# First stage of a two-block kernel: the copies of the turned tables and ScalarE's sign of them become two steps a round apart, modulation goes ahead of the powers, weights are split one step ahead

## The chip, the cores and the metric

One core of a Trainium2 chip runs the whole program; the other seven are idle. The metric is device microseconds (us) of one execution. The engines are PE (TensorE, matmuls), DVE (VectorE), ACT (ScalarE), POOL (GpSimd) and SP (SyncE, which issues nearly all DMAs). Each works through its own instructions in order and waits on semaphores.

## What is computed

Two transformer-like blocks on 512 positions of 1,024 channels in float32. The change lies in the first mixer of the first block, a state-space mixer (S5), and in the work before it:

```python
def modulate(x, g, shift, scale):
    return rmsnorm(x, g) * (1.0 + scale) + shift
...
    u = h @ w_in
...
    lb_re = mag * jnp.cos(lim * dt)
    lb_im = mag * jnp.sin(lim * dt)
...
    def chunk_step(carry, u_c):
        bu_re = jnp.einsum('blgc,gpc->blgp', u_c, bb_re)
...
        _, _, hs_re, hs_im = lax.associative_scan(combine, (a_re, a_im, bu_re, bu_im), axis=1)
        y = jnp.einsum('blgp,gcp->blgc', hs_re, cr) - jnp.einsum('blgp,gcp->blgc', hs_im, ci)
```

There are 64 groups of 16 channels, each with 64 complex states. Later come a gated output, a gated MLP, attention, and a second block with two more attentions and MLPs; nothing of that is touched.

## The kernel before

**The first stage** (the block that begins at line 729) treats the 64 groups in eight units of eight groups. Positions are taken eight at a time, so that the recurrence has 64 steps with the eighth power of the state's factor. A unit n passes through steps, each named by a letter and the unit's number:

- W splits the unit's slice of `s5_w_in` into a high part (`whi`, ACT, L271) and a low part (`wlo`, POOL, L272; unit 0's on DVE); G is the projection of 24 matmuls (L378 to L380, three products of eight slices), its copy `sq` (ACT, L921) and the store `ud` (SP); L loads it back as `U`.
- K (ACT, L951 to L955) signs the unit's constants; F (DVE, L979 to L984) and C (POOL, L967 to L969) make its two tables `bt` and `cp`.
- P (PE, L1004) turns `bt`, and ACT copies it to `bp` (L1005); Q (PE, L1013 and L1016; ACT `lags`, L1018) and A (eight DMAs, L1023) make the table `T` of short lags.
- R makes rotations for two units (DVE, L934 to L936, six operations); **U** (`turns`, L986 to L997) copies a unit's rotations to both halves of the partitions, tile `ecs` (two DMAs of 256 KB, L993), and then ACT signs the half `es` (L994) and fills `d` for the scan (L997).
- I (PE, L1034; ACT, L1037) is the input to the states; **S** (DVE, L1044 to L1047: a product with `ec`, one with `es`, a sum, the scan; ACT, L1050: exchange of halves; DVE, L1052) the recurrence; B (DVE, L1058 and L1059) turns the states back; O (PE, L1067 and L1069; ACT, L1072, the gelu `dg`; a store) is the output.

The order of all these steps is written out by hand in the string ORDER (L76), one line for each round, and a loop (L1168) issues them; PE, DVE and POOL keep that order, ACT keeps it within this block. SP's queue is put in order by the framework's scheduler. In round n stand S, B and O of unit n, and P, Q, A and I of unit n+1, beside W of n+4 and G of n+3:

```python
         "S1 W5 F3 B1 C3 P2 G4 Q2 A2 I2 O1 U3 L3 K4 "
         "S2 W6 F4 B2 C4 P3 G5 Q3 A3 I3 O2 R2 U4 L4 K5 "
```

Tiles rotate through few buffers: two of `ecs`, of `whi`, of `wlo` and of PSUM `mm`, three of PSUM `s`.

**Ahead of the rounds**, DVE makes the exponentials and sines; the constants of the input table (`den` to `kim`, L834 to L846); the normalised input `hnl` (L854); the eighth power of `mag` (L860); and from it the powers of the rotations, `up` (L871 to L875). Then come the modulation's `m_ada` and `A` (L1109, L421), and for each of eight slices `split_x` (ACT L901 and L905, DVE L903 and L906), which gives the operands of G0. Beside the splits the table `few` of small rotations is built, by a list `lf` of operations that are merged between them (recorded operations all have line L721). POOL makes the powers `LR`, `LI`, then `KR`, `KI` (L1106 to L1108), then C of unit 0.

**After the rounds** the gated output goes on with `cb`, a broadcast of `c` that takes over the buffer of `few` (load L125, silu on ACT L126).

Of the kernel before, what the change touches and what calls it, by code (L numbers as in the profile page):

```python
# [9 lines left out]
F32 = mybir.dt.float32  # L10
F32R = mybir.dt.float32r
I32 = mybir.dt.int32
AF = mybir.ActivationFunctionType
OP = mybir.AluOpType
# [4 lines left out]
P = 128  # L19
D = 1024  # L20
S = 512
KD = D // P
# [6 lines left out]
C1 = 6.28125  # L29
C2 = 0.0019350051879882812  # L30
C3 = TWO_PI - C1 - C2
# [21 lines left out]
def _consts():  # L53
# [19 lines left out]
C_DVE, BC_BUFS = 0, 3  # L73
Z_POOL, W_ADD, SUMS_POS, SPREAD_POS, GATE_RATE = 0, 'dve', 12, 22, 1.3
T_ACT, MERGE_AT = 0, 50
ORDER = ("G0 W1 G1 F0 L0 P0 K1 W2 R0 G2 Q0 A0 C1 F1 L1 W3 U0 I0 U1 K2 "  # L76
# [8 lines left out]
LAG_BUFS, U_BUFS, U_ACT, W_DVE, LO_POOL, BC_POS, XR, NORM_POOL, V_DVE, SP_ORDER = 2, 3, 0, 0, 0, 4, 0, 8, 0xaa, 2  # L85
EARLY = 6
# [5 lines left out]
def tile_two_blocks(ctx, tc, ap, out):  # L92
    nc = tc.nc
    pe, act, dve, pool = nc.tensor, nc.scalar, nc.vector, nc.gpsimd

    hp = ctx.enter_context(tc.tile_pool(name="hp", bufs=1))
    hnp = ctx.enter_context(tc.tile_pool(name="hnp", bufs=KD))
# [4 lines left out]
    ps_mm = ctx.enter_context(tc.tile_pool(name="ps_mm", bufs=2, space=PSUM))  # L102
# [313 lines left out]
    h = [hp.tile([P, S], F32, name=f"h{k}") for k in range(KD)]  # L416
# [306 lines left out]
    def merge(*lists):  # L723

        todo = sorted(((i + 0.5) / len(l), n, i) for n, l in enumerate(lists) for i in range(len(l)))
        for _, n, i in todo:
            lists[n][i]()

    with tc.block(schedule_with_timeline_sim=TIMELINE):
# [39 lines left out]
        def part(i):  # L769
            k, j = divmod(i, 4)  # L770
            raw = hnp.tile([P, S], F32, name="hnh")
            nc.sync.dma_start(raw, ap["ada_w0"][k * P:(k + 1) * P, j * S:(j + 1) * S])
            pe.matmul(rows[32 * j:32 * j + 32], cz[:, k, :], raw, start=k == 0, stop=k == KD - 1)
        norm, ln = Norm(KD, pool), Later(dve)
# [14 lines left out]
        def sm(n):  # L789
            return sc.tile([P, NG], F32, name="sm_" + n)  # L790
        dt, mag, th, x, x2 = sm("dt"), sm("mag"), sm("th"), sm("x"), sm("x2")
# [39 lines left out]

        KR, KI = (sc.tile([P, NG, 8], F32, name=n) for n in ("KR", "KI"))
        kre, kim, den, nre = sm("kre"), sm("kim"), sm("den"), sm("nre")
        dve.tensor_tensor(den, lre, lre, OP.mult)  # L834
        dve.tensor_tensor(x2, lim, lim, OP.mult)
        dve.tensor_tensor(den, den, x2, OP.add)
# [8 lines left out]
        dve.tensor_tensor(kim, kim, x2, OP.subtract)  # L845
        dve.tensor_tensor(kim, kim, den, OP.mult)  # L846

        for i in range(SUMS_POS, SPREAD_POS):
            part(i)
        rb = norm.spread(ps_mm, "mm")  # L850
        hs = []
        for k in range(KD):
            t = hnp.tile([P, S], F32, name="hnl")
            dve.tensor_tensor(t, h[k], rb, OP.mult)  # L854
            hs.append(t)

        for _ in range(3):
            dve.tensor_tensor(mag, mag, mag, OP.mult)  # L860
        pows = [sc.tile([P, 3, NG], F32, name=f"up{i}") for i in range(3)]
        for half in range(2):
            r = HALF[half]
# [2 lines left out]
            act.activation(to[:, 0], cs3[r, 1:3, gs], AF.Copy)  # L866
            act.activation(to[:, 1], sn3[r, 1:3, gs], AF.Copy, scale=-1.0)
            act.activation(to[:, 2], sn3[r, 1:3, gs], AF.Copy)
        ut = sm("ut")
        for c, nx in zip(pows, pows[1:]):  # L870
            dve.tensor_tensor(ut, c[:, 2, :], c[:, 2, :], OP.mult)  # L871
            dve.tensor_tensor(nx[:, 0, :], c[:, 0, :], c[:, 0, :], OP.mult)
            dve.tensor_tensor(nx[:, 0, :], nx[:, 0, :], ut, OP.subtract)
            for j in (1, 2):
                dve.scalar_tensor_tensor(nx[:, j, :], c[:, 0, :], 2.0, c[:, j, :], op0=OP.mult, op1=OP.mult)  # L875
# [20 lines left out]
        def split_x(k):  # L896
            hi, lo = hnp.tile([P, S], F32R, name="hnh"), hnp.tile([P, S], F32R, name="hnl")
            X.append((hi, lo))
            a, b = A[:, k:k + 1], B[:, k:k + 1]
            v = tmp.tile([P, S], F32, name=f"t{k % 4}")  # L900
            act.activation(hi, hs[k], AF.Identity, bias=b, scale=a)  # L901
            if V_DVE >> k & 1:
                dve.tensor_scalar(v, hs[k], a, b, op0=OP.mult, op1=OP.add)  # L903
            else:
                act.activation(v, hs[k], AF.Identity, bias=b, scale=a)  # L905
            (pool if LO_POOL >> k & 1 else dve).tensor_tensor(lo, v, hi.bitcast(F32), OP.subtract)  # L906
# [34 lines left out]
        class Tables:  # L941
# [44 lines left out]
            def turns(self):  # L986
                i = self.i
                e = E[i % 4]
                ecs = sp.tile([P, 2, G8, 64], F32, name="ecs")
                self.ec, self.es = ecs[:, 0], ecs[:, 1]  # L990
                src = HALF[i // 4]
                for r in HALF:
                    nc.sync.dma_start(ecs[r], e[src])  # L993
                act.activation(self.es, self.es, AF.Identity, scale=sgn[:, 0:1])  # L994
                self.d0 = d0s[order.index(i) % 2]
                gs = slice(i * G8, (i + 1) * G8)
                act.activation(self.d0[:, :, 1:], mag[:, gs, None].to_broadcast([P, G8, 63]), AF.Copy)  # L997
# [87 lines left out]
        tabs, U = [], []  # L1085
        bsp = ps_a.tile([P, S], F32, name="aux")
        tabs.append(Tables(0))
        lf = Later(dve)
        et = ps_s.tile([P, 2, NG, 4], F32, name="s")
        lf.memset(few[:, 0, :, 0:1], 1.0)  # L1090
        lf.memset(few[:, 1, :, 0:1], 0.0)
# [11 lines left out]
        for x, y, z, op in ((KR, kre, kim, OP.subtract), (KI, kim, kre, OP.add)):  # L1103
            sh = [P, NG, 8]
            t = tmp.tile(sh, F32, name="t0")
# [7 lines left out]
        split_x(1)  # L1113
        wt = split_w(0, dve)
        tabs[0].for_c(pool)
        for x, y in zip(turn_by, pows):
            act.activation(x, y, AF.Copy)
        merge([lambda k=k: split_x(k) for k in range(2, KD)], lf.ops)
        weights_of, sab, wz, w_of, wg = {0: wt}, {}, {}, {}, {}
        tabs, U = [tabs[0]] + [None] * (KD - 1), [None] * KD  # L1120
        Y, glu = [None] * KD, {}
# [33 lines left out]
        def do_glu(m, i):  # L1155
            if not i:
                glu[m] = ps_mm.tile([P, S], F32, name="mm")
            k = order[i]
            cs_ = slice(k * P, (k + 1) * P)
            mm3(glu[m], wg[m][0][:, cs_], wg[m][1][:, cs_], *Y[k], i == 0, i == KD - 1)  # L1160
# [1 line left out]
            "K": do_tables, "F": lambda n: tabs[n].for_b(dve), "C": lambda n: tabs[n].for_c(dve if C_DVE >> n & 1 else pool),  # L1162
            "W": do_w, "G": lambda n: gather(n, weights_of.pop(n)), "P": lambda n: tabs[n].on_pe(), "Q": lambda n: tabs[n].for_lags(), "L": do_u,
            "I": do_inputs, "S": do_states, "B": do_back, "A": lambda n: tabs[n].toeplitz(), "O": do_outputs,
            "R": do_rotations, "U": lambda n: tabs[n].turns(), "Y": do_y, "v": do_glu_w,
            "a": lambda i: do_glu(0, i), "b": lambda i: do_glu(1, i),
        }
        for step in ORDER.split():  # L1168
            steps[step[0]](int(step[1]))
# [12 lines left out]
        for m in range(KD):  # L1182
# [7 lines left out]
            y = tmp.tile([P, S], F32, name="t1")  # L1190
# [4 lines left out]
        norm = Norm(KD)  # L1195
# [70 lines left out]
    norm = nxt  # L1266
# [99 lines left out]
    norm = Norm(KD)  # L1366
# [19 lines left out]
    norm = nxt  # L1386
# [3 lines left out]
    W2 = ap["a_wqkv_2"]  # L1390
# [36 lines left out]
    norm = Norm(KD)  # L1427
# [25 lines left out]
    norm = nxt  # L1453
# [126 lines left out]
    norm = Norm(KD)  # L1580
# [138 lines left out]
```

## Time and profile before

| | us |
|---|---|
| median of 3 runs (2684.5, 2689.98, 2694.06) | 2689.98 |
| the profiled execution | 2683.22 |
| its span, first to last instruction | 2681.3 |
| busy in the span: PE / DVE / ACT / POOL | 2519.2 / 1737.9 / 1148.6 / 357.4 |

PE is busy for 94% of the span. In the page's 40 slices of 67 us it has 4, 8, 7 and 6 tenths in the first four and 9 in nearly all that follow, and the clock that TensorE was granted is 8, 7, 8 and 6 tenths of full speed in these four and 9 later. So the first 270 us are where PE waits, and they are read by stretches, by the waits there, and by the instructions in order of time.

### The profile page before, as it was taken

The numbers are of one execution on the slowest core, as the hardware profiler recorded it, in microseconds if no ns is written. First come the engines' busy times: TensorE is split into PE (matmuls) and PEld (weight loads), VectorE is DVE, ScalarE is ACT, GpSimd is POOL, SyncE is SP. The second block draws the span as 40 slices with busy tenths as digits, with TensorE's granted clock in tenths as the row PEclk, the third lists the DMA queues.
The fourth block names the chain that finished last, engine by engine and source line by source line (L and its number), as shares of the span: only waits on it lengthen the run. The fifth ranks groups of instructions, "written<-read, shape, count | busy, mean of one in ns | idle before, by whom it ended". The sixth has DMA issues, their size and how long they took to land. (4 is left out here: it accounts for less than half of the span.)

```text
span 2681.3 us, 32817 instructions
## 1 busy us (share of the span) xinstructions
PE 2519.2 (94%) x12098; PEld 2015.6 (75%) x12098; DVE 1737.9 (65%) x3111; ACT 1148.6 (43%) x1925; POOL 357.4 (13%) x346
## 2 busy tenths in 40 slices
PE   4876989999999999999999999999999889999998
PEld 1665778888877767888887877788888667788887
DVE  8654886455577668646568566985766776753554
ACT  3443344233355554323335554532434576542342
POOL 4441100000022210000012110550000220000000
PEclk8786989999999999999999999999999899999999
DMA  5443655354433235546433333455543112223322
GB/s 207 114 118 103 214 194 164 113 164 132 121 102 103 91 122 158 166 147 194 146 117 118 97 109 126 146 153 169 173 141 109 31 32 87 87 85 105 95 82 75
DMA packets 131120, 335.67 MB, mean 125 GB/s; under 512 B 37008, under 2 KB 41872, under 8 KB 130960
## 3 DMA queue, kind: packets, MB, share of 16 engines
q1 hardware_dynamic: 129232, 331.74, 40.3%
q8 instruction: 95, 1.56, 0.2%
q10 hardware_dynamic: 1728, 1.84, 0.2%
q14 instruction: 65, 0.53, 0.1%
HBM read 320.68 MB, written 6.29 MB: 122 GB/s over the span
## 5 line engine op out<-in xcount | busy, mean ns | idle before, releaser
L272 DVE TENSOR_TENSOR wlo<-wraw,whi 128x1024 fp32r<-128x1024 f32 (+4 forms) x424 | 464.5, 1096 | 419.6 <-ACT whi L271 414.1
L271 ACT ACTIVATE whi<-wraw 128x1024 fp32r<-128x1024 f32 (+4 forms) x431 | 408.0, 948 | 744.7 <-PE mm L379 551.0
L378 PE MATMUL mm<-hnh,whi 128*128 128x512 f32 x1152 | 467.3, 406 | 33.4 <-ACT whi L271 22.0
L379 PE MATMUL mm<-hnl,whi 128*128 128x512 f32 x1152 | 462.9, 402 | 9.0 <-POOL hnl L296 4.0
L380 PE MATMUL mm<-hnh,wlo 128*128 128x512 f32 x1152 | 459.6, 399 | 4.8 <-POOL wlo L272 3.9
L378 PE MATMUL mm<-g,whi 128*128 128x512 f32 (+1 forms) x922 | 360.1, 391 | 6.3 <-ACT g L271 3.1
L380 PE MATMUL mm<-g,wlo 128*128 128x512 f32 (+1 forms) x922 | 359.3, 390 | 0.0
L379 PE MATMUL mm<-g,whi 128*128 128x512 f32 (+1 forms) x922 | 359.2, 390 | 0.0
L378 PE MATMUL s<-hnh,whi 128*128 128x512 f32 x720 | 288.2, 400 | 0.0
L379 PE MATMUL s<-hnl,whi 128*128 128x512 f32 x720 | 285.4, 396 | 0.0
L380 PE MATMUL s<-hnh,wlo 128*128 128x512 f32 x720 | 283.9, 394 | 0.0
L378 PEld LDWEIGHTS mm<-hnh,whi 128*128 128x128 f32 x1152 | 219.2, 190 | 85.8 <-ACT whi L271 23.3
L379 PEld LDWEIGHTS mm<-hnl,whi 128*128 128x128 f32 x1152 | 219.3, 190 | 65.8 <-POOL hnl L296 9.1
L380 PEld LDWEIGHTS mm<-hnh,wlo 128*128 128x128 f32 x1152 | 218.8, 190 | 56.9 <-POOL wlo L272 5.5
L136 DVE SCALAR_TENSOR_TENSOR ada<-ada,cb 128x1024 f32<-128x1024 f32 x192 | 239.4, 1248 | 9.5 <-DMA ada<-in_ada_w_dram 9.2
L378 PEld LDWEIGHTS mm<-g,whi 128*128 128x128 f32 x922 | 173.6, 188 | 45.4 <-ACT g L271 3.8
L379 PEld LDWEIGHTS mm<-g,whi 128*128 128x128 f32 x922 | 173.9, 189 | 37.6 <-DVE g L277 0.7
L380 PEld LDWEIGHTS mm<-g,wlo 128*128 128x128 f32 x922 | 173.8, 189 | 37.5 <-issue 0.8
L380 PEld LDWEIGHTS s<-hnh,wlo 128*128 128x128 f32 x720 | 135.3, 188 | 32.5 <-issue 0.7
L378 PEld LDWEIGHTS s<-hnh,whi 128*128 128x128 f32 x720 | 135.5, 188 | 30.2
L379 PEld LDWEIGHTS s<-hnl,whi 128*128 128x128 f32 x720 | 135.6, 188 | 29.5 <-issue 0.5
L591 ACT ACTIVATE p<-p,nb 128x128 f32<-128x128 f32 x192 | 105.6, 551 | 69.3 <-DVE nb L586 41.7
(415 smaller groups left out, 3722.0 us busy)
## 6 DMA issues: line engine op xcount, KB each, us to landing
ada<-in_mod_w_dram SPq DMA_DIRECT2D x96, 512.0 KB, 4.1
wraw<-in_ffn_w_up_dram SPq DMA_DIRECT2D x88, 512.0 KB, 3.6
wraw<-in_f_win_dram SPq DMA_DIRECT2D x88, 512.0 KB, 3.5
ada<-in_ada_w_dram SPq DMA_DIRECT2D x80, 512.0 KB, 4.3
wraw<-in_ffn_w_down_dram SPq DMA_DIRECT2D x32, 384.0 KB, 3.2
wraw<-in_f_wout_dram SPq DMA_DIRECT2D x32, 384.0 KB, 3.1
wraw<-in_ffn_w_down_dram SPq DMA_DIRECT2D x32, 320.0 KB, 2.9
wraw<-in_f_wout_dram SPq DMA_DIRECT2D x32, 320.0 KB, 2.9
```

Of the source, the lines that this page charges most:

```text
L136: dve.scalar_tensor_tensor(raw, raw, 1.0, cb, op0=OP.mult, op1=OP.mult, accum_out=dst[:, i:i + 1])
L271: act.activation(hi, v, AF.Copy)
L272: return eng.tensor_tensor(lo, v, hi.bitcast(F32), OP.subtract)
L378: pe.matmul(ps, wh, xh, start=start, stop=False)
L379: pe.matmul(ps, wh, xl, start=False, stop=False)
L380: return pe.matmul(ps, wl, xh, start=False, stop=stop).ins
L591: act.activation(p[:, sl], p[:, sl], AF.Exp, bias=nb[:, qb:qb + 1], scale=scale, accum_out=l[:, qb:qb + 1])
```

## The change

Three parts, all in the first stage.

1. **U becomes two steps.** `turns` (U) keeps the two DMAs; a new step u (`turn_signs`) has ACT's sign and the filling of `d`. In ORDER, U of unit n+2 moves up behind B of unit n, and u of unit n+1 stands where U of unit n+2 stood.
2. **Modulation, then powers.** The normalised input is made ahead of `den` to `kim`; `mag`'s eighth power, the powers `up` and their three copies to PSUM go into the list `lf`, that is, between the splits.
3. **Weights one ahead.** W1 stands ahead of G0, W2 ahead of G1, W3 ahead of G2. R0, U0 and U1 move ahead of G2.

```diff
-ORDER = ("G0 W1 G1 F0 L0 P0 K1 W2 R0 G2 Q0 A0 C1 F1 L1 W3 U0 I0 U1 K2 "
-         "S0 W4 F2 B0 C2 P1 G3 Q1 A1 I1 O0 R1 U2 L2 K3 "
-         "S1 W5 F3 B1 C3 P2 G4 Q2 A2 I2 O1 U3 L3 K4 "
...
+ORDER = ("W1 G0 W2 G1 F0 L0 P0 K1 R0 U0 U1 W3 G2 Q0 A0 C1 F1 L1 I0 u0 K2 "
+         "S0 W4 F2 B0 R1 U2 C2 P1 G3 Q1 A1 I1 O0 u1 L2 K3 "
+         "S1 W5 F3 B1 U3 C3 P2 G4 Q2 A2 I2 O1 u2 L3 K4 "
...
+        for i in range(SUMS_POS, SPREAD_POS):
+            part(i)
+        rb = norm.spread(ps_mm, "mm")
+        hs = []
+        for k in range(KD):
+            t = hnp.tile([P, S], F32, name="hnl")
+            dve.tensor_tensor(t, h[k], rb, OP.mult)
+            hs.append(t)
         dve.tensor_tensor(den, lre, lre, OP.mult)
...
-        for _ in range(3):
-            dve.tensor_tensor(mag, mag, mag, OP.mult)
...
                 for r in HALF:
                     nc.sync.dma_start(ecs[r], e[src])
+
+            def turn_signs(self):
+                i = self.i
                 act.activation(self.es, self.es, AF.Identity, scale=sgn[:, 0:1])
...
         lf = Later(dve)
+        for _ in range(3):
+            lf.tensor_tensor(mag, mag, mag, OP.mult)
+        ut = sm("ut")
+        lf.ops.append(lambda: act.activation(turn_by[0], pows[0], AF.Copy))
+        for i, (c, nx) in enumerate(zip(pows, pows[1:])):
+            lf.tensor_tensor(ut, c[:, 2, :], c[:, 2, :], OP.mult)
...
+            lf.ops.append(lambda i=i: act.activation(turn_by[i + 1], pows[i + 1], AF.Copy))
...
-        for x, y in zip(turn_by, pows):
-            act.activation(x, y, AF.Copy)
```

PE's instructions stand in the same order as before in the whole program. DVE's differ only ahead of F0, POOL's only in that W3's `wlo` comes before C1. After the first stage no engine's order differs.

On ACT, where G0's end, the next splits and the first input step stand, before (`whi_635` is W1's, `whi_700` W2's, `sq_631` and `sq_666` the copies of G0 and G1, `bp_683` P0's):

```order
L901 ACTIVATE hnh_599<-hnl_431,m_ada00_132,A_s5_522 128x512
L921 ACTIVATE sq_631<-mm_606 128x512
L271 ACTIVATE whi_635<-wraw_493 128x1024
L921 ACTIVATE sq_666<-mm_641 128x512
L1005 ACTIVATE bp_683<-pt_684 128x512
```

and now (`whi_606` is W1's, `whi_641` W2's, `sq_637` and `sq_672` the copies of G0 and G1):

```order
L891 ACTIVATE hnh_597<-hnl_418,m_ada00_132,A_s5_509 128x512
L271 ACTIVATE whi_606<-wraw_479 128x1024
L911 ACTIVATE sq_637<-mm_612 128x512
L271 ACTIVATE whi_641<-wraw_527 128x1024
L911 ACTIVATE sq_672<-mm_647 128x512
```

Each high part moves ahead by the copy of one projection.

On ACT, the end of round 0 before: behind the gelu of O0 (`dg_961`) stands the sign of `ecs_973`, the third `ecs` tile, which is unit 2's and which S2 reads, and behind it the exchange of S1:

```order
L1072 ACTIVATE dg_961<-s_944 128x512
L994 ACTIVATE ecs_973<-ecs_973,cc_87 128x512
L997 ACTIVATE d00_124<-sm_mag_180 128x8x63
L951 ACTIVATE bc_980<-bc_980,cc_87 128x128
L952 ACTIVATE bc_980<-bc_980 128x128
L954 ACTIVATE aux_507<-bc_980 128x128
L955 ACTIVATE aux_507<-bc_980,cc_87 128x128
L1050 ACTIVATE s_941<-s_932 64x512 x2
```

and now: the sign there is of `ecs_717`, unit 1's, which the S1 behind it reads:

```order
L1065 ACTIVATE dg_970<-s_953 128x512
L987 ACTIVATE ecs_717<-ecs_717,cc_87 128x512
L990 ACTIVATE d01_125<-sm_mag_180 128x8x63
L941 ACTIVATE bc_978<-bc_978,cc_87 128x128
L942 ACTIVATE bc_978<-bc_978 128x128
L944 ACTIVATE aux_493<-bc_978 128x128
L945 ACTIVATE aux_493<-bc_978,cc_87 128x128
L1043 ACTIVATE s_950<-s_941 64x512 x2
```

The instructions are the same; the unit that they serve is one earlier.

One thing of another stage moves, on ACT at the end of round 4: before, the silu of `cb` (with its table load) stood behind the `bp` copies that follow S5's exchange:

```order
L955 ACTIVATE aux<-bc,cc 128x128
L1050 ACTIVATE s<-s 64x512 x2
L1005 ACTIVATE bp<-pt 128x512 x2
L126 ACT_TABLE_LOAD
L126 ACTIVATE cb<-cb 128x1024
L1018 ACTIVATE lags<-pt 16x512 x2
```

and now ahead of that exchange:

```order
L944 ACTIVATE aux<-bc 128x128
L126 ACT_TABLE_LOAD
L126 ACTIVATE cb<-cb 128x1024
L945 ACTIVATE aux<-bc,cc 128x128
L1043 ACTIVATE s<-s 64x512 x2
L998 ACTIVATE bp<-pt 128x512 x2
```

So the table load, which waits for the load of `cb`, and the silu now come ahead of S5's exchange and of P6's copies.

## Rows read from the trace of the kernel before

**Rows 1.** Busy time by stretch; per engine busy us (count), granted clock, DMA share, GB/s.

```profile
105.00:211.00 106.00, 79.17 (x545) 68.50 (x543) 66.44 (x103) 44.76 (x86) 49.65 (x36) 0.83 0.50 128
```

**Rows 2.** Waits from 45 to 272 us: us in total, times, longest us.

```profile
PE pt L1013 <- ACT bp L1005: 35.2, 7, 9.4
...
ACT ecs L994 <- DMA ecs<-ada: 26.3, 5, 7.8
...
PE mm L378 <- ACT whi L271: 22.0, 4, 16.1
```

**Rows 3.** ACT in order of time: start, us, instruction, idle before it.

```profile
104.81 1.17 ACT L1050 ACTIVATE s<-s 64x512 f32<-64x512 f32 x2 [1.00 <-DVE s L1047]
...
120.02 0.60 ACT L1072 ACTIVATE dg<-s 128x512 f32<-128x512 f32 x1 [5.79 <-PE s L1069]
124.69 0.72 ACT L994 ACTIVATE ecs<-ecs,cc 128x512 f32<-128x512 f32 x1 [4.07 <-DMA ecs<-ada]
...
127.14 1.17 ACT L1050 ACTIVATE s<-s 64x512 f32<-64x512 f32 x2
...
190.25 1.17 ACT L1050 ACTIVATE s<-s 64x512 f32<-64x512 f32 x2
...
210.58 1.17 ACT L1050 ACTIVATE s<-s 64x512 f32<-64x512 f32 x2
```

**Rows 4.** DVE in order of time: S0, B0, rotations of round 0, S1.

```profile
102.09 0.69 DVE L1045 TENSOR_TENSOR s<-s,ecs 128x512 f32<-128x512 f32 x1
...
112.21 0.69 DVE L1059 TENSOR_TENSOR t<-t,s 128x512 f32<-128x512 f32 x1
...
113.58 1.65 DVE L935 TENSOR_TENSOR sqa<-cb 128x512 f32<-128x512 f32 x1
...
119.85 0.68 DVE L1044 TENSOR_TENSOR t<-s,ecs 128x512 f32<-128x512 f32 x1
```

**Rows 5.** PE in order of time: first of Q1, of O0, of O1, last of O1, first of Q3.

```profile
107.48 0.39 PE L1013 MATMUL pt<-cp,bt 128*16 128x128 f32 x2 [0.54 <-ACT bp L1005]
...
112.95 0.63 PE L1067 MATMUL s<-U,T 128*128 128x64 f32 x2 [1.23 <-DVE t L1059]
...
135.47 0.39 PE L1067 MATMUL s<-U,T 128*128 128x64 f32 x2
...
138.82 0.39 PE L1069 MATMUL s<-t,cp 128*128 128x63 f32 x2
...
149.88 0.38 PE L1013 MATMUL pt<-cp,bt 128*16 128x128 f32 x2 [4.27 <-ACT bp L1005]
```

**Rows 6.** DVE ahead of the rounds, in order of time.

```profile
53.52 0.17 DVE L1109 TENSOR_TENSOR m_ada<-pt,vec 128x16 f32<-128x16 f32 x1
...
68.56 0.69 DVE L906 TENSOR_TENSOR hnl<-t,hnh 128x512 fp32r<-128x512 f32 x1
```

**Rows 7.** POOL: W1's low part, and one operation of C2.

```profile
71.69 2.35 POOL L272 TENSOR_TENSOR wlo<-wraw,whi 128x1024 fp32r<-128x1024 f32 x1 [18.82 <-ACT whi L271]
...
113.07 1.61 POOL L967 TENSOR_TENSOR cp<-LR,bc 128x576 f32<-128x576 f32 x1
```

**Rows 8.** PE ahead of the rounds: first of G1 and its third product, G2, Q0.

```profile
71.66 0.51 PE L378 MATMUL mm<-hnh,whi 128*128 128x512 f32 x1 [1.63 <-ACT whi L271]
...
74.09 0.79 PE L380 MATMUL mm<-hnh,wlo 128*128 128x512 f32 x1 [1.55 <-POOL wlo L272]
...
85.32 0.50 PE L378 MATMUL mm<-hnh,whi 128*128 128x512 f32 x1 [2.82 <-ACT whi L271]
...
95.25 0.39 PE L1013 MATMUL pt<-cp,bt 128*16 128x128 f32 x2
```

**Rows 9.** The load of cb: SP's issue, then ACT's table load, then its landing.

```profile
206.83 0.72 SPq L125 DMA_DIRECT2D cb<-in_c_dram  x1
...
212.76 1.28 ACT L126 ACT_TABLE_LOAD   x1
...
DMA to landing us min/median/max: 5.1/5.1/5.1
```

More of the change, by code (lines that the diff above doesn't have):

```diff
@@ L846, in tile_two_blocks @@
         dve.tensor_tensor(kim, kim, den, OP.mult)
[L848 to L855, printed above, removed]
-        for _ in range(3):
-            dve.tensor_tensor(mag, mag, mag, OP.mult)
         pows = [sc.tile([P, 3, NG], F32, name=f"up{i}") for i in range(3)]
@@ L868, in tile_two_blocks @@
             act.activation(to[:, 2], sn3[r, 1:3, gs], AF.Copy)
[L869 to L875, printed above, removed]
         up = [ps_s.tile([P, S], F32, name="s") for _ in range(2)]
@@ L1088, in tile_two_blocks @@
         lf = Later(dve)
+        for _ in range(3):
[4 more added lines that the diff above has]
+            lf.tensor_tensor(ut, c[:, 2, :], c[:, 2, :], OP.mult)
+            lf.tensor_tensor(nx[:, 0, :], c[:, 0, :], c[:, 0, :], OP.mult)
+            lf.tensor_tensor(nx[:, 0, :], nx[:, 0, :], ut, OP.subtract)
+            for j in (1, 2):
+                lf.scalar_tensor_tensor(nx[:, j, :], c[:, 0, :], 2.0, c[:, j, :], op0=OP.mult, op1=OP.mult)
+            lf.ops.append(lambda i=i: act.activation(turn_by[i + 1], pows[i + 1], AF.Copy))
         et = ps_s.tile([P, 2, NG, 4], F32, name="s")
@@ L1164, in tile_two_blocks @@
             "I": do_inputs, "S": do_states, "B": do_back, "A": lambda n: tabs[n].toeplitz(), "O": do_outputs,
-            "R": do_rotations, "U": lambda n: tabs[n].turns(), "Y": do_y, "v": do_glu_w,
+            "R": do_rotations, "U": lambda n: tabs[n].turns(), "u": lambda n: tabs[n].turn_signs(), "Y": do_y, "v": do_glu_w,
             "a": lambda i: do_glu(0, i), "b": lambda i: do_glu(1, i),
```

10 rows, old and new, of the table ORDER are left out of this document.

## The prediction

> **What bounds the kernel now.** I read the page's slices first (PE is full after 270 us, so only the first stage can give or lose much), then the waits between 45 and 272 us, then ACT, DVE, PE and POOL there in order of time. From 105 to 211 us, rounds 0 to 4 in the main, PE is busy 79 of 106 us at a granted clock of 0.83 [rows 1]. Its largest wait is for ACT's `bp` copies, 35.2 us in seven waits; ACT's largest is for the copies into `ecs`, 26.3 us in five [rows 2]. One round shows how they hang together [rows 3]: the gelu of O0 starts at 120.02, the sign of the next copy only at 124.69 after 4.07 us of waiting for the DMA, the exchange of S1 at 127.14. DVE's scan of S1 was long done: nothing but place in ACT's queue kept the exchange, the weights' split and `bp` back, and PE waited for `bp` (4.27 us before Q3 [rows 5]). I call T_n the start of S_n's exchange (L1050). T0 is 104.81, T1 127.14, T4 190.25, T5 210.58 [rows 3]: five rounds in 105.8 us, 21.15 each; rounds 0 to 3 take 85.4, round 4 20.3.
>
> Ahead of the rounds PE waits 22.0 us for `whi` [rows 2]: 16.1 before G0, then 1.63 and 2.82 before G1 and G2, each of these followed by 1.55 for POOL's `wlo` (one of the two rows shown) [rows 8].
>
> **The change part by part.**
>
> *Modulation, then powers.* The first split follows `m_ada`, which runs at 53.52 [rows 6]. Some 9.5 us of `mag` and powers leave from ahead of it, and the normalised input no longer waits for `kim`, so I put `m_ada` near 42 and PE's first matmul 11 us earlier (estimates). But G0 ends with the last low part, at 68.56 [rows 6], and up to there DVE hardly idles; the moved operations run between the splits instead. So the cover is gone at the other end: worth nothing by itself. It can also cost. POOL is idle for the 18.82 us before W1's `wlo` [rows 7], that is, during today's splits; in the new order `KR` follows a later `kre`, and some ten POOL operations of 1.1 us fall among the splits. What that does is seen in round 0: beside C2 a DVE sum of 0.69 takes 1.65 [rows 4], and POOL's operation 1.61 [rows 7]. Today the same contention lies on the powers and costs about 6 us there. I take G0's end 1.5 later than its 70.0, because W1's `wlo` of 2.35 [rows 7] now runs among the last splits; bounds 3 earlier to 5 later.
>
> The Trainium skill, page "SBUF — State Buffer", section "Who interferes with whom", says that a VectorE instruction with two SBUF inputs and a GpSimd instruction that reads SBUF exclude each other, the later one waiting for the whole of the other. The trace agrees (1.65 for 0.69). It speaks against this part: ten operations of 1.1 us would put G0's end 11 us later, less the 6 paid today: 5 instead of 1.5, and the sum below would be a gain of 17.8.
>
> *Weights one ahead.* Both pairs of waits go: W1's parts are made during G0, W2's during G1, on ACT and POOL, idle there. G1 loses 3.2, G2 4.4. G1 stays as slow as it is without its wait, about 8.5, for G0 is still starved; P0 takes 1.0. G2 took 9.9 from 85.32 to 95.25 [rows 8], mostly at the lower of the two clock levels; it now follows without a gap, and I take 5.6, as at the upper level (P and G together take 6.4 between O1's end at 139.2 and the wait that ends at 149.88 [rows 5]). So 71.5 + 8.5 + 1.0 + 5.6 = 86.6 for Q0 instead of 95.25: 8.6 earlier. From Q0 to T0 it takes 9.6; W3's high part no longer stands there and the exchange of I0 goes ahead of the sign: 0.8 less. T0 comes **9.4 earlier**, bounds 3 and 13.
>
> *The sign a round later.* U's copies now have a whole round; the five waits of 26.3 go. What is late next is not the old wait's neighbour but a loop, since the sign behind O_n's gelu is now the one that S_(n+1) needs:
> - T_n to the end of B_n: 112.21 + 0.7 - 104.81 = 8.1 [rows 3, 4], with F between; then O can start. PE is there by then: Q1 starts 2.7 after T0, and Q and I took 4.2 at the upper level (107.48 to 112.95 - 1.23) [rows 5].
> - O: 3.6 at the upper level (135.47 to 138.82 + 0.39), about 6.8 at the lower (112.95 to 119.8, the gelu following at 120.02) [rows 3, 5].
> - gelu 0.2 later, sign 0.5 after its start and 0.75 to DVE's product with `es` (estimates from 0.60 and 0.72), from there 2.72 to the exchange (102.09 to 104.81) [rows 3, 4]: 4.2.
>
> Together 16.0 or 19.2. PE's own work, Q to G, is shorter than that: P and G (6.4) fit into the 7.0 from O's end to the next Q. In rounds 0 and 2 the rotations lie between B and S on DVE: 112.9 to 119.85 [rows 4] beside C on POOL, which gives 8.1 + 7.0 + 0.6 + 2.7 = 18.3, or 19.2 with a slow O. Rounds 0 to 3: 68.6 if every O is fast, 76.8 if every one is slow, against 85.4. PE will still pause for about 1 us before O (8.1 against 6.9), and O0, which came after 1.23 us of waiting, was slow, while O1 was fast; I take the middle, 72.7: **12.7 gained**, bounds 8.6 and 16.8.
>
> *The load of `cb`.* Round 4 gets a new wait. ACT's table load and silu now stand ahead of S5's exchange and wait for `cb`, whose buffer is free when the rotations of round 4 end, 8.1 + 3.9 = 12.0 after T4 (six operations at 0.65, an estimate: POOL is through with C6 by then). SP reaches it there: behind eight copies into `T` and two loads, about 12.3. Landing takes 5.1, the table load 1.28 [rows 9], silu and one small operation 1.4 (an estimate): T5 = T4 + 20.0, against 20.3. So round 4 gains **0.3**, bounds -2 and 3 (if SP is late, or the landing shorter), though its ACT wait for `ecs` goes. Queued behind it are `bp` of P6 and PE.
>
> *Past round 4* nothing shortens: S6 waits for the outputs' loads and splits. In round 6 the last sign and fill now stand ahead of ACT's splits: **1.1 lost**.
>
> In PE's, DVE's and POOL's other orders nothing moves; SP's copies are issued earlier, between the `T` copies, where the next `U` is not needed for a further 4 us; that costs nothing unless SP itself becomes late by as much.
>
> **Sum:** 9.4 + 12.7 + 0.3 - 1.1 = 21.3 us gained, all before 272 us, and PE-bound work after it passes that on whole. The profiled execution took 2683.2, which is 6.8 below the median; the four executions shown average 2687.9, and I subtract from that: **2666.6**, or 2667.
>
> **The rivals.**
> 1. *Half of it.* POOL's operations among the splits put T0's gain at 3, every O runs at the lower level (8.6), and `cb` lands late (-1): 3 + 8.6 - 1 - 1.1 = 9.5, 2678. For it: PE keeps a pause before each O. Against it: O1 to O4 were fast beside longer pauses elsewhere.
> 2. *More.* All O fast, no slower splits, `cb` earlier: 12 + 16.8 + 3 - 1.1 = 30.7, 2657. Against it: the splits do get POOL's company.
> 3. *It does not do what it says:* SP comes to the copies so late that ACT still waits for them. Then only the front gains, about 9: 2679. Against it: in the built order the copies stand at most three `T` copies behind B's end, a whole round ahead of their sign.
> 4. *Slower: the clock.* A round is now one closed loop through PE, ACT and DVE. At the upper level PE's work in it is O 3.6, Q and I 4.2, P and G 6.4: 14.2. If its pauses keep TensorE at the lower level all the time, that is 28.4, 7.2 more than today's 21.15: 36 lost in five rounds, 6 gained in front, 2718. It decides where the granted clock of the rounds falls under 14.2/21.15 = 0.67. Against it: it is 0.83 [rows 1] with more pauses than will be left. The Trainium skill, page "TensorE: Matmul & The Clock Gate", section "HAM oscillation — how this bites in real kernels", describes such a loop that goes cold in every turn; no row here stays at the lower level for a whole round.
>
> **How the numbers follow.** Forecast 0.55, rivals 1 to 4: 0.24, 0.12, 0.05, 0.04. A measurement can tell about 0.3%, 8 us. The forecast and rival 2 are faster than that; of rivals 1 and 3, which lie at that edge (2679.9), a little more than half: 0.84 faster. Slower is rival 4 and a little for what I did not see: 0.05. The rest, 0.11, is the same. The range 2653 to 2682 takes in rivals 2, 1 and 3 with a few us for the spread of runs (2684.5 to 2694.1) and leaves out rival 4 and the tails.
>
> **What would show it.** ACT's wait for `ecs` under 3 us in all; PE's first matmul near 46, G0's end near 70 to 73; no wait of G1 and G2 for `whi` or `wlo`; T0 near 95; the rounds 0 to 3 between 68 and 77 us together; a wait of ACT's table load for the load of `cb` in round 4, with T5 - T4 near 20. I am wrong if G0 ends early (the splits were not DVE's to set), if T5 - T4 falls to 17, or if the rounds stay at 20 with the `ecs` waits gone.

## The result and the profile after

The changed kernel takes 2658.19 us (median of four executions, 2652.14 to 2663.97) beside 2689.28 of the kernel before on the same chip: a ratio of 0.9884, interval 0.9855 to 0.9913, 31 us less. The forecast was 2667, with a range of 2653 to 2682. It came out faster, as forecast, and inside the range, but the gain was put some 10 us too low: the time is nearer to rival 2's 2657.

The profiled execution is the slowest of the four (2663.97; its span is 2662.2 after 2681.3). I read it with the prediction's yardsticks: T_n, the start of S_n's exchange (now L1043), and the stage's end, the start of the first sigmoid. A second profile of the same kernel, from the first experiment below, stands beside it. The forecast's column is made from the prediction's terms.

| us | before | after | after, second profile | forecast |
|---|---|---|---|---|
| G0's copy (`sq`) | 70.07 | 72.01 | 71.48 | 71.5 |
| T0 | 104.81 | 93.52 | 94.05 | 95.4 |
| rounds 0 to 3 together | 85.4 | 71.2 | 69.6 | 72.7 |
| each of them | 22.3, 20.0, 23.0, 20.2 | 18.4, 18.2, 18.5, 16.1 | 18.9, 16.0, 18.5, 16.1 | 16.0 to 19.2 |
| round 4 (T4 to T5) | 20.3 | 20.9 | 21.7 | 20.0 |
| round 5 | 23.5 | 24.6 | 20.3 | 23.5 |
| round 6 | 19.4 | 21.2 | 21.0 | 20.5 |
| stage's end | 273.42 | 251.31 | 246.47 | 252.1 |
| span | 2681.3 | 2662.2 | 2653.9 | |

The waits between 45 and 272 us, after (engine, line waited for: us in total, times, longest). ACT's 26.3 us for the copies into `ecs` [rows 2] are gone from the list, and PE's wait for `whi` is down from 22.0 to 6.6, none of it in G1 and G2. PE waits 18.7 for `bp` where it waited 35.2 (23.0 in the second profile). New is DVE's wait for the sign (L987), the loop that the prediction named, and ACT's table load that waits for `cb`:

```profile
PE pt L1006 <- ACT bp L998: 18.7, 4, 9.0
DVE s L1038 <- ACT ecs L987: 13.0, 3, 6.2
PE mm L379 <- DVE hnl L896: 7.5, 5, 2.8
PE mm L378 <- ACT whi L271: 6.6, 2, 4.1
ACT L126 <- DMA cb<-in_c_dram: 0.4, 1, 0.4
```

ACT in order of time, after. The copies of G0, G1 and G2 (L911) come 6.3 and 6.4 apart; they were at 70.07, 81.66 and 95.36 before. The sign now follows O0's gelu at once (106.91), and between it and the next exchange ACT waits 2.62 us for DVE's scan, not 4.07 for a DMA ahead of the sign [rows 3]:

```profile
72.01 0.60 ACT L911 ACTIVATE sq<-mm 128x512 f32<-128x512 f32 x1 [4.83 <-PE mm L380]
78.33 0.60 ACT L911 ACTIVATE sq<-mm 128x512 f32<-128x512 f32 x1 [4.78 <-PE mm L380]
84.71 0.60 ACT L911 ACTIVATE sq<-mm 128x512 f32<-128x512 f32 x1 [2.76 <-PE mm L380]
89.98 0.71 ACT L987 ACTIVATE ecs<-ecs,cc 128x512 f32<-128x512 f32 x1
93.52 1.17 ACT L1043 ACTIVATE s<-s 64x512 f32<-64x512 f32 x2 [1.11 <-DVE s L1040]
...
106.41 0.60 ACT L1065 ACTIVATE dg<-s 128x512 f32<-128x512 f32 x1 [3.39 <-PE s L1062]
106.91 0.71 ACT L987 ACTIVATE ecs<-ecs,cc 128x512 f32<-128x512 f32 x1
...
111.95 1.17 ACT L1043 ACTIVATE s<-s 64x512 f32<-64x512 f32 x2 [2.62 <-DVE s L1040]
```

### The profile page after: what moved, and what is told of

Same layout as the page of the kernel before. It is cut to its first block, busy times and chain, and to the rows that moved or that the text cites. A ratio compares the mean times of both kernels' runs of the same rounds, so it can differ in the third digit from the quotient of the medians.

```text
span 2662.2 us, 32825 instructions
## 1 busy us (share of the span) xinstructions
PE 2525.7 (95%) x12098; PEld 2019.1 (76%) x12098; DVE 1737.6 (65%) x3111; ACT 1149.0 (43%) x1925; POOL 359.2 (13%) x346
## 5 line engine op out<-in xcount | busy, mean ns | idle before, releaser
L378 PE MATMUL mm<-hnh,whi 128*128 128x512 f32 x1152 | 469.3, 408 | 19.3 <-ACT hnh L317 7.5
L379 PEld LDWEIGHTS mm<-hnl,whi 128*128 128x128 f32 x1152 | 219.8, 191 | 71.4 <-DVE hnl L896 11.3
L591 ACT ACTIVATE p<-p,nb 128x128 f32<-128x128 f32 x192 | 105.6, 552 | 69.8 <-DVE nb L586 41.7
```

The source lines that it names most:

```text
L378: pe.matmul(ps, wh, xh, start=start, stop=False)
L379: pe.matmul(ps, wh, xl, start=False, stop=False)
L591: act.activation(p[:, sl], p[:, sl], AF.Exp, bias=nb[:, qb:qb + 1], scale=scale, accum_out=l[:, qb:qb + 1])
```

## The experiments

All gains below are from the ratio to the kernel before, run beside each kernel on the same chip (medians 2686.0 to 2689.4 us), with its 95% interval.

| run | T0 | rounds 0 to 3 | round 4 | stage's end | median | ratio (interval) |
|---|---|---|---|---|---|---|
| after_again | 94.05 | 69.6 | 21.7 | 246.5 | 2656.1 | 0.9877 (0.9858 to 0.9896) |
| e1_rounds | 105.51 | 69.7 | 17.1 | 254.0 | 2669.2 | 0.9917 (0.9901 to 0.9934) |
| e2_weights | 94.43 | 85.3 | 20.7 | 263.6 | 2678.4 | 0.9955 (0.9939 to 0.9972) |
| e3_modul | 105.63 | 81.0 | 24.1 | 274.3 | 2687.5 | 0.9995 (0.9983 to 1.0008) |
| e4_no_modul | 93.75 | 71.1 | 22.5 | 248.6 | 2662.3 | 0.9912 (0.9893 to 0.9931) |
| e5_cb_late | 93.55 | 72.3 | 16.5 | 244.6 | 2655.5 | 0.9885 (0.9864 to 0.9905) |
| e6_c_first | 93.48 | 70.3 | 22.5 | 247.9 | 2657.6 | 0.9894 (0.9873 to 0.9915) |
| e7_c0_late | 89.05 | 70.3 | 21.3 | 241.7 | 2654.2 | 0.9875 (0.9853 to 0.9896) |
| e8_c_tu | 93.60 | 68.7 | 21.8 | 242.4 | 2656.7 | 0.9888 (0.9871 to 0.9904) |
| e9_cb_c0 | 88.99 | 71.2 | 19.3 | 243.4 | 2652.2 | 0.9878 (0.9862 to 0.9893) |
| e10_all | 88.08 | 68.7 | 17.4 | 232.7 | 2649.9 | 0.9863 (0.9845 to 0.9880) |
| e11_fill | 88.94 | 64.0 | 19.1 | 233.5 | 2645.0 | 0.9839 (0.9821 to 0.9857) |

T0 to the stage's end are of each run's one profile.

### Once more, and the parts alone

**after_again** is the changed kernel unedited.

> The changed kernel once more. Theory A (all of the gain is in the first stage, and its two profiles give 22.1 us at the stage's end and 19.1 at the span's end): 19 to 23 us faster than before, ratio 0.9915 to 0.993. Rival (the medians' 31 us is right, and something past the first stage gained too): 29 to 33 us, ratio 0.988 to 0.989.

It came out at 33 us faster (28 to 38), as the rival said in number. Its reason, a gain past the first stage, no trace shows: from the stage's end to the span's end it is 2407.9 us before and 2407.4 here. Three of its four executions took 2656, one 2663. The second profile shows what the first hid: there O1, O4 and O5 were slow (their gelus 14.1, 15.3 and 16.3 us after their T), here they come after 12.0, 13.0 and 12.0, and only O0 is later (14.9 against 12.9). The stage's end differs by 4.8 us between two executions of one kernel, most of it in round 5 (24.6 and 20.3). There the same 88 records of matmuls kept PE busy for longer where the granted clock was lower. The stretches T5 to T6 before, after and in the second profile (us; us of length; busy time of PE, PEld, DVE, ACT, POOL; then the clock, 1.00 being 2.4 GHz and 0.50 the lower level, 1.2 GHz; DMA share, GB/s):

```profile
210.58:234.06 23.48, 14.26 (x88) 12.80 (x88) 12.57 (x20) 11.65 (x17) 7.75 (x7) 0.57 0.44 112
185.59:210.19 24.60, 16.14 (x88) 14.65 (x88) 12.58 (x20) 9.42 (x16) 5.17 (x5) 0.50 0.40 97
185.34:205.62 20.28, 10.71 (x88) 9.31 (x88) 12.58 (x20) 9.43 (x16) 2.13 (x2) 0.75 0.42 94
```

Past the stage, too, executions differ with the clock; see the last section.

**e1_rounds** is the kernel before with U parted and the order's rounds of the change, its opening line kept:

```diff
-ORDER = ("G0 W1 G1 F0 L0 P0 K1 W2 R0 G2 Q0 A0 C1 F1 L1 W3 U0 I0 U1 K2 "
-         "S0 W4 F2 B0 C2 P1 G3 Q1 A1 I1 O0 R1 U2 L2 K3 "
+ORDER = ("G0 W1 G1 F0 L0 P0 K1 W2 R0 G2 Q0 A0 C1 F1 L1 W3 U0 u0 I0 U1 K2 "
+         "S0 W4 F2 B0 R1 U2 C2 P1 G3 Q1 A1 I1 O0 u1 L2 K3 "
...
+            def turn_signs(self):
```

> The kernel before with the copies of the turned tables and the sign parted and put a round apart from round 0 on; opening, modulation and weights as before. Theory A (the parts add up): T0 stays near 104.8, rounds 0 to 3 fall from 85.4 to 71 to 73, rounds 5 and 6 lose 1 to 3; 9 to 12 us faster. Rival (the short rounds rest on what the new opening put out of the way): rounds 0 to 3 near 78, 5 us faster.

22 us faster (18 to 27): theory A's mechanism, with rounds even below its 71 to 73 (69.7), and twice its total. Rounds 0 to 3 gain 15.8, round 4 3.2, round 5 3.2; round 6 loses 2.0 and T0 0.7: 19.4 at the stage's end. Rounds 4 and 5 are what I had left out. In round 4 ACT's table load and silu of `cb` stand behind the lags here, with nothing to wait for, and the exchange of S5 does not wait for them:

```profile
192.28 1.17 ACT L1053 ACTIVATE s<-s 64x512 f32<-64x512 f32 x2 [1.12 <-DVE s L1050]
193.38 1.06 ACT L1008 ACTIVATE bp<-pt 128x512 f32<-128x512 f32 x2
...
198.74 1.28 ACT L126 ACT_TABLE_LOAD   x1
200.04 1.06 ACT L126 ACTIVATE cb<-cb 128x1024 f32<-128x1024 f32 x1
```

The same place in the changed kernel (second profile): 3.55 us of waiting, and the exchange behind it.

```profile
182.71 1.28 ACT L126 ACT_TABLE_LOAD   x1 [3.55 <-DMA cb<-in_c_dram]
184.00 1.06 ACT L126 ACTIVATE cb<-cb 128x1024 f32<-128x1024 f32 x1
184.97 0.35 ACT L945 ACTIVATE aux<-bc,cc 128x128 f32<-128x128 f32 x1
185.34 1.17 ACT L1043 ACTIVATE s<-s 64x512 f32<-64x512 f32 x2
```

**e2_weights** is the kernel before with only the weights' splits moved ahead:

```diff
-ORDER = ("G0 W1 G1 F0 L0 P0 K1 W2 R0 G2 Q0 A0 C1 F1 L1 W3 U0 I0 U1 K2 "
+ORDER = ("W1 G0 W2 G1 F0 L0 P0 K1 R0 W3 G2 Q0 A0 C1 F1 L1 U0 I0 U1 K2 "
```

> The kernel before with the weights of each gather split one gather ahead and nothing else. Theory A (weights ahead carry the front, the modulation's place is worth nothing): T0 near 96, rounds as before, 8 to 9 us faster. Rival M (the front's gain comes from the modulation being earlier): T0 near 101 to 102, about 3 us faster, because the last parts of the weights come behind later splits.

12 us faster (8 to 16; theory A said 8 to 9), T0 at 94.43, rounds as before: theory A; M falls. T0's gain comes with the weights alone.

**e3_modul** is the kernel before with only the modulation moved ahead of `den` to `kim`, `mag` and the powers (with the powers among the splits; the order as before, U whole).

> The kernel before with the modulation ahead of the powers and nothing else. Theory A: G0 ends between 70 and 73, T0 104 to 107, between 0 and 2 us slower. Rival M: T0 near 98 to 101, 4 to 6 us faster.

1 us faster (5 faster to 2 slower), G0's copy at 70.66, T0 at 105.63: worth nothing by itself, as forecast. In its profile round 4 takes 24.1: there too the silu of `cb` stands ahead of S5's exchange (207.39 against 210.79). The three parts alone give 22, 12 and 1, together 36 against the change's 33: within the intervals they add up.

**e4_no_modul** is the changed kernel with that same part taken back.

> The changed kernel with the modulation put back behind the powers: the copies and signs a round apart and the weights ahead, nothing else. ACT's silu of cb then stands behind S5's exchange again, as in the kernel before. Theory A (the parts add; the modulation's place is worth nothing, and what it does cost is the place of that silu): T0 near 94.4, rounds 18.5, 16.1, 18.4, 16.1, 17.1, 20.3 and 21.4, the stage's end at 242 to 244, 2650 to 2654 us, that is 3 to 5 us faster than the changed kernel. Rival M (the modulation ahead is worth some us of the front): T0 near 97 or later, 2656 us or slower.

T0 is 93.75, as theory A says, but the silu stands early here as well (185.99, T5 at 187.33; round 4 22.5): my reason for the place of the silu was wrong. It is placed by the scheduler outside the written order, and what decides it was not found. The median is 2662.3, not 2650 to 2654. The profiled execution is the fastest of the six (2654.65, the others 2660.6 to 2666.4), so no trace shows where those lost: the time is the rival's, T0 is theory A's, and whether the modulation's place is worth a few us beside the two other parts stays open.

### What bounds the stage now

**e5_cb_late** gives the load of `cb` a place in the order:

```diff
-         "S5 F7 B5 U7 C7 P6 Q6 A6 I6 O5 Y0 u6 L7 Y1 v0 "
+         "S5 F7 B5 U7 C7 P6 Q6 A6 c0 I6 O5 Y0 u6 L7 Y1 v0 "
...
+            "c": lambda n: cbs.append(bcast_load("c")),
```

> The changed kernel with the load of cb and its silu given a place in the order behind A6, so that S5's exchange no longer stands behind them. Theory C (the silu's wait for the load is what round 4 pays): round 4 falls from 21.7 to 17.1, round 5 stays at 20.3, stage's end near 242, 2651 to 2652 us. Rival (round 4 is set by its rotations and a slow O4): round 4 stays above 20, 2655 us or more.

Round 4 falls to 16.5, so theory C holds for round 4; the whole is not faster than the changed kernel (2655.5, not 2651 to 2652). Round 3 took 18.5 instead of 16.1, its gelu 14.5 after T3, and round 6 0.9 more.

**e6_c_first** puts C ahead of W on POOL in rounds 0 to 5 (round 0 shown):

```diff
-         "S0 W4 F2 B0 R1 U2 C2 P1 G3 Q1 A1 I1 O0 u1 L2 K3 "
+         "S0 C2 W4 F2 B0 R1 U2 P1 G3 Q1 A1 I1 O0 u1 L2 K3 "
```

> The changed kernel with each round's C (POOL's products) ahead of the split of the weights on POOL, so that it is through before DVE makes the rotations. Theory L (a round is the longer of two loops: with rotations DVE's, 18.3 to 18.5, because C stretches them; without, the loop over O, 16.0): rounds 0 and 2 fall to 16 to 16.6, rounds 1 and 3 stay at 16.0 or, with a slow O, 18.2; 3 to 5 us faster than the changed kernel, 2651 to 2653. Rival (rotation rounds are set by O and the clock, not by DVE): rounds 0 and 2 stay above 18, 2656.

Rounds 0 and 2 take 16.0 and 16.2: theory L holds. But rounds 1 and 3 take 18.8 and 19.3, their gelus 14.7 and 15.3 us after T, and the sum is the changed kernel's: 70.3 against 69.6 and 71.2. The granted clock of e6 by stretches (columns as above) falls in O1 and O3:

```profile
90.00:105.00 15.00, 12.80 (x101) 11.17 (x100) 13.20 (x23) 9.45 (x18) 11.45 (x9) 1.00 0.57 143
105.00:120.00 15.00, 13.42 (x98) 11.67 (x97) 10.98 (x19) 8.72 (x17) 9.69 (x7) 0.94 0.67 176
120.00:135.00 15.00, 15.00 (x86) 13.14 (x85) 7.89 (x15) 7.18 (x15) 8.54 (x7) 0.72 0.37 97
135.00:150.00 15.00, 14.65 (x118) 13.04 (x118) 12.46 (x22) 9.17 (x18) 8.49 (x7) 1.00 0.66 168
150.00:165.00 15.00, 13.77 (x67) 12.92 (x67) 5.80 (x10) 5.28 (x13) 5.47 (x5) 0.66 0.64 166
```

PE had waited for DVE's last step of B ahead of O0, which stayed at the upper level, and of O1 and O3, which did not (PE in order of time, e6; start, us, and the wait in brackets):

```profile
101.62 0.44 PE L1060 MATMUL s<-U,T 128*128 128x64 f32 x2 [1.15 <-DVE t L1052]
...
117.62 0.44 PE L1060 MATMUL s<-U,T 128*128 128x64 f32 x2 [1.23 <-DVE t L1052]
...
152.61 0.69 PE L1060 MATMUL s<-U,T 128*128 128x64 f32 x2 [1.23 <-DVE t L1052]
```

One kernel cannot say whether the wait matters, but all 14 profiles of this case can. Take rounds 0 to 4 of each, 70 O's, and the list of clock stretches in its trace. Where PE waited 1.15 to 1.67 us right ahead of O, the clock fell in O or just before it in 30 of 34. Where it waited 0.34 or less, it fell in none of 27 (e11's first four among them). Between lie eight, with four falls; one O was at the lower level already. Without the filling of e11, 15 of 23 O's that hardly waited follow one at the lower level, so these counts alone do not part the wait from what went before; e11 does, below.

**e7_c0_late** takes POOL's C0 from among the splits:

```diff
-        tabs[0].for_c(pool)
...
-ORDER = ("W1 G0 W2 G1 F0 L0 P0 K1 R0 U0 U1 W3 G2 Q0 A0 C1 F1 L1 I0 u0 K2 "
+ORDER = ("W1 C0 G0 W2 G1 F0 L0 P0 K1 R0 U0 U1 W3 G2 Q0 A0 C1 F1 L1 I0 u0 K2 "
```

> The changed kernel with POOL's C0 behind the low part of W1 instead of among the splits. Theory D (the end of G0 is set by DVE, whose operations beside C0 take some 6 us more than alone): the last split 4 to 6 us earlier, T0 at 89 to 90 instead of 94, 2651 to 2652 us. Rival (ACT or PE sets G0's end, or W2's low part is late behind C0): T0 at 93 or later, 2655 to 2657.

Theory D holds: G0's copy at 66.08, T0 at 89.05, the stage's end at 241.7, each some 5 us earlier than in the second profile. DVE in the changed kernel, beside C0:

```profile
49.53 2.18 DVE L272 TENSOR_TENSOR wlo<-wraw,whi 128x1024 fp32r<-128x1024 f32 x1
51.63 3.79 DVE L721 TENSOR_TENSOR sm_mag<-sm_mag 128x64 f32<-128x64 f32 x3
55.35 1.66 DVE L896 TENSOR_TENSOR hnl<-t,hnh 128x512 fp32r<-128x512 f32 x1
56.94 1.43 DVE L721 TENSOR_TENSOR sm_ut<-up 128x64 f32<-128x64 f32 x1
```

and in e7, with POOL idle there:

```profile
49.06 1.21 DVE L272 TENSOR_TENSOR wlo<-wraw,whi 128x1024 fp32r<-128x1024 f32 x1
50.20 0.73 DVE L721 TENSOR_TENSOR sm_mag<-sm_mag 128x64 f32<-128x64 f32 x3
50.85 0.68 DVE L896 TENSOR_TENSOR hnl<-t,hnh 128x512 fp32r<-128x512 f32 x1
51.45 0.22 DVE L721 TENSOR_TENSOR sm_ut<-up 128x64 f32<-128x64 f32 x1
```

These four groups alone take 9.06 beside C0 and 2.84 without: 6.2 us. The rule that the prediction took from the Trainium skill, page "SBUF — State Buffer", section "Who interferes with whom", agrees. By time alone e7 (0.9853 to 0.9896) is not told from the changed kernel.

**e9_cb_c0** is e5 and e7 together.

> The changed kernel with cb's load behind A6 and C0 behind the low part of W1, both of which did in their places what was expected. Theory A (first-stage gains add up and the rest of the program passes them on): T0 near 89, round 4 near 17, stage's end at 236 to 239, 2646 to 2650 us. Rival (what is gained in one round is given back by a slow O in another, and after the stage): stage's end at 241 or later, 2653 to 2656.

T0 held (88.99); but O1, O4 and O5 were slow (14.1, 15.3 and 14.4), round 4 took 19.3, and the stage ended at 243.4: the rival, though the median, 2652.2, lies between the two. 33 us faster than before (29 to 37), the change's own gain. As in e5 and e6, the edits did in their places what was expected, and slow O's elsewhere took most of it back.

**e8_c_tu** is e6, and O starts with its eight products with T instead of taking them in turn with those with w; **e10_all** adds e5's and e7's edits. In these two the products with T and w no longer add up to the kernel's output; the instructions of O are the same, in another order.

```diff
             for g in range(G8):
-                pe.matmul(yp[:, g, :], tab.T[:, g], U[:, g, :], start=True, stop=False)
+                pe.matmul(yp[:, g, :], tab.T[:, g], U[:, g, :], start=True, stop=True)
+            for g in range(G8):
                 for x in w:
```

> The changed kernel with C ahead of the weights' split on POOL, and in O all eight products with T ahead of the eight with w, so that PE does half of O in the 1.2 us for which it waits before O. Theory K (an O at the lower clock follows PE's wait ahead of it, and gives back what the shorter rotation rounds gained): rounds 0 to 3 all between 15.5 and 16.5, 62 to 66 us together, stage's end at 241 to 244, 2650 to 2653 us. Rival (the clock falls all the same, in another place): at least one gelu 14 us or more after its T, rounds 0 to 3 together 68 or more, 2655 to 2658.

> All four edits together: cb's load late, C0 late, C ahead of the weights' split, T's products first in O. Theory A and K: T0 near 89, rounds 0 to 4 near 16 each, stage's end at 231 to 235, 2641 to 2646 us. Rival: slow O's as before, stage's end 238 or later, 2650 or more.

e8: rounds 19.3, 16.0, 17.2, 16.1, and 2656.7: the rival. But the edit had not done what it was for. The products with T do not read w, and still wait 1.15 us for B (e8, PE):

```profile
101.74 3.66 PE L1060 MATMUL s<-U,T 128*128 128x64 f32 x16 [1.15 <-DVE t L1052]
```

So the wait is for something else that B frees; I take it to be O's PSUM buffer, one of the three of `s`, of which B's last step reads one. Theory K was not tried by it. e10 ended the stage at 232.7, inside K's 231 to 235, but with rounds of 17.0, 16.3, 19.3, 16.0, O2 slow (15.3); 2649.9, above its 2646.

**e11_fill** leaves O as in the changed kernel, keeps the three other edits (C first, C0 and `cb` late) and fills PE's wait:

```diff
+            pf = ps_t.tile([P, 4, P], F32, name="pt")
+            for g in range(4):
+                pe.matmul(pf[:, g, 0:64], ident, ident[:, 0:64], start=True, stop=True)
             yp = ps_s.tile([P, G8, 64], F32, name="s")
```

> cb's load late, C0 late, C ahead of the weights' split (the three edits of e10 that leave O as it is), and four products of a constant with itself, some 1.0 us that nobody reads, ahead of each O, in the 1.15 us for which PE waits there for B (the wait is still there in e8, whose first products did not read w, so it is for the buffer that B frees). Theory K: PE's pause ahead of O is what lets the clock fall in O; no gelu later than 13 us after its T in rounds 0 to 3, rounds 0 to 3 together 63 to 66, stage's end 232 to 236, 2642 to 2647 us. Rival (the fall is not tied to that pause): rounds 0 to 3 together 68 or more, at least one of their O's at the lower clock, 2648 to 2652.

All of theory K's signs came. T0 to T4 are 88.94, 104.94, 120.94, 136.94 and 152.94: four rounds of 16.0, each gelu 12.0 after its T. The four products (two records each) take 1.06, 0.26 of the wait is left, and O0 is at the upper level (e11, PE):

```profile
95.77 1.06 PE L1060 MATMUL pt<-cc 128*128 128x64 f32 x8
97.08 0.43 PE L1063 MATMUL s<-U,T 128*128 128x64 f32 x2 [0.26 <-DVE t L1052]
97.36 0.39 PE L1065 MATMUL s<-t,cp 128*128 128x63 f32 x2
```

The granted clock of e11 in the stretches that were shown of e6:

```profile
90.00:105.00 15.00, 13.70 (x114) 12.26 (x114) 14.00 (x23) 9.04 (x18) 9.38 (x7) 1.00 0.66 154
105.00:120.00 15.00, 14.31 (x117) 12.73 (x116) 8.98 (x17) 8.66 (x17) 8.69 (x7) 1.00 0.62 161
120.00:135.00 15.00, 14.31 (x118) 12.71 (x117) 12.69 (x23) 7.96 (x15) 8.71 (x8) 1.00 0.51 139
135.00:150.00 15.00, 14.31 (x117) 12.78 (x116) 9.07 (x16) 7.72 (x15) 9.69 (x7) 1.00 0.63 158
150.00:165.00 15.00, 14.23 (x99) 12.60 (x98) 13.10 (x23) 6.81 (x15) 7.38 (x6) 0.88 0.51 131
```

In round 4 0.77 of the wait is left, and there the clock falls again, in O4:

```profile
161.10 0.43 PE L1063 MATMUL s<-U,T 128*128 128x64 f32 x2 [0.77 <-DVE t L1052]
161.74 0.64 PE L1063 MATMUL s<-U,T 128*128 128x64 f32 x2
```

So with the pause filled, and no slow O before, none of four O's fell; in the kernels without the filling 30 of 34 did after that pause. That ties the fall to the pause, in rounds 0 to 3; the products also give PE 1 us more of work in each round, and that is not parted from it.

What it is worth in time is less clear. After the fall in O4 e11's clock stays low from 161.4 to 178.5, and rounds 4 to 6 take 61.8 against e10's 58.8; the stage ends at 233.5, no earlier than e10's 232.7. e11 takes 2645.0 us (2643.5 to 2649.5), ratio 0.9839 (0.9821 to 0.9857): 43 us faster than before (38 to 48). All five executions are below all eight of the changed kernel (2652.1 to 2664.0), beside medians of the kernel before of 2687.1 and of 2689.3 and 2689.4; the changed kernel's intervals are 0.9858 to 0.9896 and, in its first measurement, 0.9855 to 0.9913. That is the four edits together. e11 without its products was not run; e10 (0.9845 to 0.9880) comes nearest and is not told from it, so the products' own share of the time is not shown.

## Why the prediction was right, and where it was off

- **What bounds the kernel:** right. The order on ACT set the rounds, and the copies' wait went whole.
- **Modulation, then powers:** worth nothing by itself (e3), as forecast. G0's end came 1.4 to 1.9 later against 1.5, and it comes with the weights, as the reason given with that number has it (W1's low part among the last splits): it is 1.7 later in e2, where only the weights move, and 0.6 in e3, where only the modulation does. So most of this term belongs to the weights. What the earlier start could bring is lost to POOL's C0 among the splits: with C0 out of the way (e7) G0's copy comes at 66.08, 4.0 earlier than before. The row of 1.65 that the prediction read as a sum is a product of the rotations; without POOL beside it, it takes 0.68 (e6), so the reading of contention stands. e4 leaves open whether the modulation is worth some us beside the rest.
- **Weights one ahead:** T0 10.8 and 11.3 earlier, forecast 9.4. The term that was mis-sized is G1: I kept it "as slow as it is without its wait, about 8.5, for G0 is still starved"; it took 6.3 and, in the second profile, 7.4. PE was busy through all of it, at a granted clock of 0.87 and 0.74. P0 and G2, 6.6 in the forecast, took 6.4.
- **The sign a round later:** gained 14.2 and 15.9, forecast 12.7 with bounds 8.6 and 16.8. The loop's sums fit to a few tenths: 16.0 to 16.5 with a fast O, 18.4 to 19.3 in rounds with rotations beside C, 18.1 to 19.3 with a slow O, against 16.0, 18.3 and 19.2 (the terms shown add up to 15.9, 18.4 and 19.1); rounds 2 of e8 and 0 of e10, with an O slow in part, took 17.2 and 17.0. The number of slow O's was a guess, the middle between none and all, and it changes from execution to execution: that 12.7 came near is in part luck. That the rotation rounds are DVE's and C's, e6 shows; that the others are O's, e11.
- **The load of `cb`:** the mechanism was right (the table load waits, the exchange behind it); round 4 loses 0.5 and 1.4 where I said 0.3 gained. The term that was off is the landing: SP issued the load 11.7 after T4 (forecast 12.3), but it landed 6.5 and 7.3 us later, not 5.1. In the first profile a slow O4 hid most of that: ACT waited only 0.4. Without the silu there, round 4 takes 16.5 to 17.4 where O4's gelu comes 12.5 to 13.4 after T4 (e1, e5, e10), and 19.1 and 19.3 with a slow O4 (e11, e9).
- **"Past round 4 nothing shortens":** this step failed. Round 5 took 23.5 to 23.9 in the three profiles with the old order of rounds (before, e2, e3) and 20.2 to 20.9 in nine of the eleven with the new one; the other two took 22.7 and 24.6. By the rows of round 5 above, its length goes with the granted clock of the whole round; why the new order keeps it higher there was not found. Round 6 lost 1.8 and 1.5, forecast 1.1.
- **The sum:** 21.3 forecast; the stage's end came 22.1 and 27.0 earlier in the two profiles. In the first: 11.3 + 14.2 - 0.5 - 1.1 - 1.8 = 22.1, near the forecast because front and rounds 0 to 3 gained 3.4 more and the later rounds 2.6 less: luck. In the second: 10.8 + 15.9 - 1.4 + 3.2 - 1.5 = 27.0.
- **Subtracting from the mean of four executions:** the medians give 31 and 33. The rest is in no profile here: the kernel before's own profiled execution was 6.1 below the median of its runs (2683.2 against 2689.3), and no trace shows where its other executions lost that.
- **The rivals:** in number rival 2 (2657) was nearest. In the second profile T0 came near its 12 and the rounds near its 16.8; its earlier `cb` did not come. Rivals 1 and 3 fell: T0, O's and ACT's wait say no. Rival 4, the loop that stays at the lower level, fell for rounds 0 to 3, whose sum came out near the forecast's, but it is near to what costs: O after O falls, if not all, and in the first profile the clock stayed at 0.50 from 172.6 to 217.0 us, the whole of round 5, which then took 24.6. The rule cited there from the Trainium skill, page "TensorE: Matmul & The Clock Gate", section "HAM oscillation — how this bites in real kernels", agrees in kind: a wait in the loop, then work at the lower level; here not in each turn.

## What to carry to other kernels

Where the order on an in-order engine puts a wait for a DMA ahead of a step that others need, part the copy from its use and put a round between them; then work out the loop that is left, leg by leg, at both levels of TensorE's clock. In a loop that PE nearly fills, a gain in one round can come back as a product run at the lower level in the next: look at the granted clock of each round before believing that an edit was worth nothing, and try a few products that nobody reads in PE's short waits (here they evened out four rounds; their worth in the whole time was not shown). An operation that the scheduler places, as `cb`'s silu here, can land in the middle of a loop; give it a place by hand.

## What the runs showed that I had not expected

- After a wait of PE of only 1.15 or 1.23 us ahead of O the clock fell within O (O1 and O3 of e6, O0 of e8 and of the second profile); not each time, for O0 of e6 had the same wait and stayed up (30 of 34 fell in all profiles). With 1.06 us of idle products in the wait it stayed at 1.00 from 90 to 150 us, and the rounds were equal to the hundredth.
- Past the stage the program is the same in all kernels, and takes 2404.3 to 2414.8 us in the 14 profiles. The trace's list of clock stretches puts 48.6 to 69.8 us of it at the lower level; less half of that, all 14 lie between 2378.0 and 2383.5. The half is an estimate, from PE's being busy for 97% of it and from O's taking 3.6 us at the upper level and 6.8 at the lower. By it the spread falls from 10.5 to 5.5 us, so about half of it goes with the clock, as much as several edits here were worth; the rest stays open. Two whole stretches, before and e7 (stage's end to the span's end, 56.0 and 69.4 us at the lower level), show it in PE's busy time, 6.9 us apart for the same instructions:

```profile
273.42:2681.30 2407.88, 2336.12 (x11068) 1876.91 (x11068) 1568.41 (x2776) 1046.35 (x1738) 251.25 (x247) 0.99 0.40 124
```

```profile
241.72:2655.80 2414.08, 2343.01 (x11068) 1881.70 (x11068) 1568.50 (x2776) 1046.25 (x1738) 250.37 (x247) 0.99 0.40 124
```

- Three DVE operations of 128x64 took 3.79 us beside POOL's C0, and 0.73 without.
